# One gate/up pair of three FFNs moved from plain products to seven products

## The chip, the core and the metric

The kernel runs on one core of a Trainium2 chip. The time is that of one execution on the device in microseconds (us); of several executions the median counts. The engines named below are TensorE (PE; its weight loads are PEld), VectorE (DVE), ScalarE (ACT), GpSimd (POOL) and SyncE (SP).

## What is computed

Two layers, each with a half-step FFN, a mixer (a gated linear recurrence and a windowed attention side by side) and a second half-step FFN. Only the FFNs matter here:

```
def rms_norm(x, gain):
    y = x * rsqrt(mean(x * x, axis=-1, keepdims=True) + 1e-6)
    return y * gain

def swiglu(h, w_gate, w_up, w_down):
    return (silu(h @ w_gate) * (h @ w_up)) @ w_down

for l in range(2):
    h = rms_norm(x, gn[0])
    x = x + 0.5 * rms_norm(swiglu(h, w_ffn1_gate[l], w_ffn1_up[l], w_ffn1_down[l]), gn[1])
    ...                                          # the mixer
    h = rms_norm(x, gn[4])
    x = x + 0.5 * rms_norm(swiglu(h, w_ffn2_gate[l], w_ffn2_up[l], w_ffn2_down[l]), gn[5])
```

x is 512 tokens by 1024 channels, gate and up are 1024 by 2816, down is 2816 by 1024, all float32. There are four FFNs.

## The kernel before

**Precision.** Every float32 operand is split into two float32r parts, `hi` and `lo`, and a product is three matmuls: hi with hi, hi with lo, lo with hi (`mm3`, all on line 115 through `mm`). Weights are the stationary operand of the gate/up products, tokens the moving one.

**Pairs.** The 2816 columns of gate and of up are 22 blocks of 128; block j of gate and block j of up are a pair, whose 512 results each become one block of the hidden vector. A pair is made in one of two ways.

- Plain: eight blocks of 128 channels for gate and eight for up, three matmuls each, 512 tokens wide: 48 matmuls. The first two pairs run together in `quad`, further ones through two calls of `project`, and `gated` (lines 909 and 910) makes silu(gate) times up.
- Seven products (`sevenths`, line 850): the channels and the tokens are halved, gate and up are the two column blocks, and seven products of quarter size take the place of eight. Each is four blocks of three matmuls, 256 tokens wide: 84 matmuls in all. Their order on PE is product 1, 2, 5, 7, 6, 3, 4. Results are put together on DVE: line 874 after product 6, lines 876 and 881, line 882 after product 4; ACT's Silu of line 894 and DVE's line 895 then give the hidden block.

`PLAIN` says how many pairs are plain in the three FFNs behind the first (the first has `FIRST`); the others take seven products. `fast` runs the pairs from `PLAIN` to 21 in a loop.

**Weights.** `Stream` brings them. A raw block of 128 by 1024 (512 KB) comes by SP's queue into one of four buffers (`w32`) and is split into `whi` and `wlo`, for which there are six buffers each. A plain pair is two items of kind u, whose `lo` DVE computes (line 331). A pair of seven products is four items out of two raw blocks:

- a (products 1 and 2): a raw block. ACT writes hi (line 324) and minus w into lo (line 328), then POOL issues a DMA that adds w to it (line 329).
- b (products 5 and 7): DVE makes two sums of weights (lines 311 and 312), ACT casts hi, DVE computes lo (line 331).
- c (products 6 and 4): the same with lines 317 and 318.
- d (product 3): half a raw block, its lo by ACT and a DMA of 256 KB, like a's.

Each item is prepared some items ahead of its use (`AHEAD` is 3).

**Tokens.** The products 5, 6, 3 and 7 need sums of token quarters. `Pre.sums` makes those of one pair of channel blocks: line 563 twice, lines 458 to 465, and a split of two tiles (ACT line 400, DVE line 401). Four calls fill `x56` and `x37`, and product 5 of the first pair needs all four. Two are called after `quad`, one ahead of each further plain pair.

**Order.** PE's instructions run in the order of the program. That of DVE, ACT, POOL and SP is chosen by the tile framework's scheduler when the kernel is built, apart from those under `pin`. An engine works through its list in order, and an instruction that waits holds up all behind it.

Of the kernel before, what the change touches and what calls it, by code (L numbers as in the profile page):

```python
# [33 lines left out]
    head=2600.0, level=1720.0, chunks=1270.0, blocks=350.0, norm=2370.0, gate=8000.0,  # L34
    values=1200.0, scores=2000.0, exp=9000.0, shares=4500.0, turn=1900.0, turned=3000.0, rest=1200.0, lent=3500.0, apart=4000.0, block=2000.0, pair=4000.0, att0=1260.0, att1=12300.0,
)
W32, WS, AHEAD, TAIL, PLAIN, FIRST, EARLY, LATE = 4, 6, 3, 4, 4, 7, 4, 8
TURN = 0
LEAD = 8
ORDER = ("p1", "p6", "p2", "p7", "p5", "p4", "p3")  # L40
# [5 lines left out]
def trunk(ctx: ExitStack, tc: tile.TileContext, xin, wall, gains, lbT, hgain, sinks, c_dist, c_mask, c_ident, out):  # L46
# [16 lines left out]
    def big(dt=F32, shape=None):  # L63
        return sb.tile(shape or [P, S], dt, tag="s", name=nm("s"), bufs=SLOTS)
# [750 lines left out]
    def quad(pre, halves):  # L815

        o = [acc() for _ in range(4)]
        blocks = {}
        ws.pinned = halves
        for half in (0, 1) if halves else (None,):  # L820
            c = WHOLE if half is None else HALF[half]
            for k in range(KT):
                order.until(lambda: pre.have[half or 0] > k)
                for j in range(4):
                    if (k, j) not in blocks:
                        blocks[k, j] = ws.next(uses=2 if halves else 1)
                    wmm(o[j][:, c], blocks[k, j], cut(pre.h[k], c), k == 0, k == KT - 1)
            ws.pinned = False
        return o

    def project(pre):
        o = acc()
        for k in range(KT):
            wmm(o, ws.next(), pre.h[k], k == 0, k == KT - 1)
        return o
# [49 lines left out]
    def fast(pre, a, start):  # L885
        def early():
            if j == FT - 1:
                for i in range(EARLY):
                    a[i] = split(a[i])

        for j in range(start, FT):
            m = sevenths(pre, early)
            z = big(F32, [P, 2, H2])
            nc.scalar.activation(out=m[:, 0:2, :], in_=m[:, 0:2, :], func=AF.Silu)  # L894
            nc.vector.scalar_tensor_tensor(z, m[:, 0:2, :], -1.0, m[:, 2:4, :], op0=ALU.mult, op1=ALU.mult)
            a.append(z.rearrange("p i t -> p (i t)"))

    def ffn(l, n, pre, nxt, halves=True):
        a = []

        def gated(og, ou):
            z, u = big(), big()
            if first:
                pin(nc.vector.tensor_tensor(z, og, pre.rb, op=ALU.mult))
                nc.scalar.activation(out=z, in_=z, func=AF.Silu)
                nc.vector.tensor_tensor(u, ou, pre.rb, op=ALU.mult)
                nc.vector.tensor_tensor(u, u, z, op=ALU.mult)
            else:
                nc.scalar.activation(out=z, in_=og, func=AF.Silu)
                pin(nc.vector.tensor_tensor(u, ou, z, op=ALU.mult))  # L910
            a.append(u)

        first = isinstance(pre, First)
        o = quad(pre, halves)
        if first:
            o.append(project(pre))
            order.until(lambda: pre.rb is not None)
        if not first:
            pre.sums()
            pre.sums()  # L920
        for j in range(2):
            gated(o[2 * j], o[2 * j + 1])
        if first:
            gated(o[4], project(pre))
            for j in range(3, FIRST):
                if j > 3:
                    order.until(lambda: pre.laid)
                    pre.sums()
                if j == 4:
                    pre.sums()  # L930
                gated(project(pre), project(pre))
            fast(pre, a, FIRST)
        else:
            for j in range(2, PLAIN):
                pre.sums()
                gated(project(pre), project(pre))
            fast(pre, a, PLAIN)
        return down(a, FT, l, n + 1, nxt, True)
# [349 lines left out]
    pre = First()  # L1288
# [69 lines left out]
    for l in range(DEPTH):  # L1358
        pre = ffn(l, 0, pre, (l, 2), halves=l > 0)
        pre = mixer(l, pre, (l, 4))  # L1360
        pre = ffn(l, 4, pre, (l + 1, 0) if l + 1 < DEPTH else None)
# [81 lines left out]
```

## Time and profile before

| | |
|---|---|
| median of 3 runs | 2113.25 us (2112.46 to 2113.26) |
| the profiled execution | 2114.98 us, of which the profile's span is 2113.2 us |
| busy share of the span | PE 99%, PEld 89%, DVE 73%, ACT 53%, POOL 7% |
| granted TensorE clock | 0.998 |
| DMA | 298.36 MB, 141 GB/s in the mean |

In the profile L115 is line 115 of the kernel. A row of the timeline has the start in us from the span's start, the length in us, engine, line, operation, the tile written, the tile read, and in brackets the idle time ahead of it with what ended it. A matmul's length includes its way through the array, so the distance between starts counts, not the length.

### The profile page before, as it was taken

Reading aid. Unit: us, or ns where it says so; the run is one execution under the profiler, and the core shown is the slowest. Engines: PE = TensorE matmul, PEld = TensorE weight load, DVE = VectorE, ACT = ScalarE, POOL = GpSimd, SP = SyncE. Lnnn points to the kernel's source line nnn. Section 1 sums busy time; section 2 is a strip of 40 time slices with the busy share of each in tenths; the row PEclk is TensorE's granted clock in tenths of the full one; section 3 lists DMA queues with packets and bytes.
Section 4 is the critical chain, followed back from the end, with each engine's and each line's share of the span. In section 5 each row is a group of like instructions: output and inputs, shape, how many; then the busy total and the mean of one; then the engine's idle time right before and its main releaser. Section 6 shows DMA issues by size and latency. Waiting matters only on the chain.

```text
span 2113.2 us, 35244 instructions
## 1 busy us (share of the span) xinstructions
PE 2101.1 (99%) x13549; PEld 1875.3 (89%) x13549; DVE 1551.0 (73%) x2705; ACT 1124.9 (53%) x1900; POOL 154.6 (7%) x188
## 2 busy tenths in 40 slices
PE   9999999999999999999999999999999999999998
PEld 7899988887888999998899998888778989999987
DVE  5777886767676777779587778767686767777884
ACT  6555554446445555556355556454554545555562
POOL 0111000000000011110001110000000000111000
PEclk9999999999999999999999999999999999999999
DMA  7577754321237357774437775632122553677651
GB/s 234 150 181 181 188 146 137 106 70 61 70 100 209 120 125 175 180 194 125 160 109 175 181 185 150 189 116 95 51 71 70 135 185 110 154 182 181 183 165 45
DMA packets 148072, 298.36 MB, mean 141 GB/s; under 512 B 16992, under 2 KB 74816, under 8 KB 147904
## 3 DMA queue, kind: packets, MB, share of 16 engines
q1 hardware_dynamic: 122416, 228.16, 32.8%
q0 software_dynamic: 25344, 67.91, 18.5%
q8 instruction: 106, 1.74, 0.3%
q14 instruction: 62, 0.51, 0.1%
q10 hardware_dynamic: 144, 0.05, 0.0%
HBM read 213.43 MB, written 14.73 MB: 108 GB/s over the span
## 4 chain that ended last, share of the span: by engine, by line
PE 81%; DVE 9%; ACT 5%; issue 2%; DMA 2%; SPq 1%; ACTq 0%; DVEq 0%
PE acc L115 60%; PE aux L115 19%; ACT whi L324 2%; DMA w<-wall 2%; PE aux L125 1%; DVE s L401 1%; DVE wlo L331 1%; DVE wlo L286 1%; PE acc L125 1%; ACT s L400 1%; ACT m L894 1%; ACT wlo L328 1%; SPq L241 1%; DVE tt L268 0%; DVE w L267 0%
## 5 line engine op out<-in xcount | busy, mean ns | idle before, releaser
L115 PE MATMUL acc<-s,whi 128*128 128x256 f32 (+1 forms) x4968 | 1069.9, 312 | 1.7 <-ACT whi L324 0.9
L115 PEld LDWEIGHTS acc<-s,whi 128*128 128x128 f32 x4968 | 809.9, 191 | 54.5 <-issue 2.1
L115 PE MATMUL acc<-s,wlo 128*128 128x256 f32 (+1 forms) x2484 | 770.5, 310 | 0.1
L115 PEld LDWEIGHTS acc<-s,wlo 128*128 128x128 f32 x2484 | 474.5, 191 | 25.9 <-DVE wlo L331 0.4
L324 ACT CAST whi<-w 128x1024 fp32r<-128x1024 f32 (+1 forms) x341 | 317.4, 949 | 252.2 <-PE aux L115 103.4
L115 PE MATMUL acc<-whi,s 128*128 128x512 f32 x1264 | 413.6, 393 | 0.0
L324 ACT CAST whi<-tt 128x1024 fp32r<-128x1024 f32 x154 | 161.7, 1050 | 341.4 <-DVE tt L318 188.9
L331 DVE TENSOR_TENSOR wlo<-w,whi 128x1024 fp32r<-128x1024 f32 (+1 forms) x181 | 218.5, 1216 | 134.8 <-ACT whi L324 128.4
L115 PEld LDWEIGHTS acc<-whi,s 128*128 128x128 f32 x1264 | 237.0, 188 | 55.7 <-issue 3.2
L331 DVE TENSOR_TENSOR wlo<-tt,whi 128x1024 fp32r<-128x1024 f32 x154 | 188.2, 1222 | 102.5 <-ACT whi L324 102.5
L115 PE MATMUL acc<-wlo,s 128*128 128x512 f32 x632 | 246.8, 391 | 1.0 <-DVE wlo L286 1.0
L329 POOL DMA_DIRECT2D wlo<-w x160 | 138.2, 865 | 1266.3 <-ACT wlo L328 856.7
L115 PE MATMUL aux<-s,whi 128*128 128x256 f32 x1232 | 225.1, 283 | 0.0
L115 PE MATMUL aux<-whi,s 128*128 128x512 f32 x592 | 196.8, 390 | 0.0
L115 PEld LDWEIGHTS aux<-s,whi 128*128 128x128 f32 x1232 | 192.2, 192 | 0.0
L115 PE MATMUL aux<-s,wlo 128*128 128x256 f32 x616 | 174.4, 283 | 0.1
L115 PEld LDWEIGHTS acc<-wlo,s 128*128 128x128 f32 x632 | 118.7, 188 | 25.8 <-DVE wlo L286 2.4
L115 PEld LDWEIGHTS aux<-whi,s 128*128 128x128 f32 x592 | 111.1, 188 | 22.9
L328 ACT ACTIVATE wlo<-w 128x1024 fp32r<-128x1024 f32 (+1 forms) x160 | 129.9, 845 | 0.0
L400 ACT CAST s<-s 128x512 fp32r<-128x512 f32 (+1 forms) x164 | 88.6, 581 | 65.9 <-DVE s L459 60.6
L115 PEld LDWEIGHTS aux<-s,wlo 128*128 128x128 f32 x616 | 118.3, 192 | 0.3 <-DMA wlo<-w 0.3
L115 PE MATMUL aux<-wlo,s 128*128 128x512 f32 x296 | 115.2, 389 | 0.0
(185 smaller groups left out, 2136.6 us busy)
## 6 DMA issues: line engine op xcount, KB each, us to landing
w<-wall SPq DMA_DIRECT2D x267, 512.0 KB, 3.7
wlo<-w POOLq DMA_DIRECT2D x83, 512.0 KB, 5.5
w<-wall SPq DMA_DIRECT2D x288, 128.0 KB, 3.1
wlo<-w POOLq DMA_DIRECT2D x77, 256.0 KB, 3.3
x_d<-s SPq DMA_DIRECT2D x48, 256.0 KB, 2.1
s<-x_d SPq DMA_DIRECT2D x48, 256.0 KB, 5.5
w<-wall SPq DMA_DIRECT2D x34, 256.0 KB, 2.9
s<-wall SPq DMA_DIRECT2D x64, 128.0 KB, 3.5
```

The source lines that it names most:

```text
L115: nc.tensor.matmul(o, lhsT, rhs, start=start, stop=stop)
L125: nc.tensor.transpose(o, src, ident)
L241: nc.sync.dma_start(w.rearrange("p (m c) -> p m c", m=4) if c is None else w[:, c], a)
L286: nc.vector.tensor_tensor(it.lo[:, h[c]], w[c], it.hi[:, h[c]].bitcast(F32), op=ALU.subtract)
L324: i = nc.scalar.copy(it.hi[:, c], w[:, c])
L328: nc.scalar.mul(it.lo[:, c], w[:, c], -1.0)
L329: nc.gpsimd.dma_start(it.lo[:, c].bitcast(F32), w[:, c], accum_op=ALU.add)
L331: nc.vector.tensor_tensor(it.lo[:, c], w[:, c], it.hi[:, c].bitcast(F32), op=ALU.subtract)
L400: nc.scalar.copy(hi, src)
L401: nc.vector.tensor_tensor(lo, src, hi.bitcast(F32), op=ALU.subtract)
L894: nc.scalar.activation(out=m[:, 0:2, :], in_=m[:, 0:2, :], func=AF.Silu)
```

## The change

`PLAIN` goes from 4 to 3: in each of the three FFNs behind the first, pair 3 takes seven products. Two calls of `Pre.sums` that stood ahead of two plain pairs now both stand ahead of the only one.

```
-W32, WS, AHEAD, TAIL, PLAIN, FIRST, EARLY, LATE = 4, 6, 3, 4, 4, 7, 4, 8
+W32, WS, AHEAD, TAIL, PLAIN, FIRST, EARLY, LATE = 4, 6, 3, 4, 3, 7, 4, 8
...
             for j in range(2, PLAIN):
-                pre.sums()
+                while len(pre.x56) < min(4, 2 * j):
+                    pre.sums()
                 gated(project(pre), project(pre))
             fast(pre, a, PLAIN)
```

The stream of weights follows from `PLAIN` (`ws.plain(min(2 * p, 8))`, `ws.pairs(FT - p)`): two items u fewer and one set a, b, c, d more in each of the three.

## The prediction

> **What bounds the kernel now.** I read the page first, then the chain that ended last, then the timeline of each engine around the place of the change in the second FFN.
>
> ```profile
> PE 2101.1 (99%) x13549; PEld 1875.3 (89%) x13549; DVE 1551.0 (73%) x2705; ACT 1124.9 (53%) x1900; POOL 154.6 (7%) x188
> PE 81%; DVE 9%; ACT 5%; issue 2%; DMA 2%; SPq 1%; ACTq 0%; DVEq 0%
> wlo<-w POOLq DMA_DIRECT2D x83, 512.0 KB, 5.5
> wlo<-w POOLq DMA_DIRECT2D x77, 256.0 KB, 3.3
> ```
>
> PE is never idle to speak of, so matmuls that go are worth their full time, as long as what feeds PE keeps its lead. The last two rows are the accumulating DMAs that finish `wlo` of items a and d: 5.5 and 3.3 us from POOL's issue to landing.
>
> ```profile
> 725.83 43.37 PE acc L115 x276
> 769.19 2.88 PE aux L115 x24
> 772.07 7.20 PE acc L115 x60
> ...
> 740.05 0.63 PE L115 MATMUL acc<-s,whi 128*128 128x512 f32 x2
> 761.84 0.40 PE L115 MATMUL acc<-s,whi 128*128 128x256 f32 x2
> ```
>
> The first three rows are of the chain: quad, both plain pairs and the first seven products pass without a gap, and a pair of seven products takes 7.20 + 2.88 = 10.08 us (84 matmuls, 0.12 us apart). The other two are of PE's timeline: the plain pairs 2 and 3 run from 740.05 to 761.84, 10.9 us each (48 matmuls, 0.227 us apart, 10.88).
>
> The lead is the question. This is DVE and ACT in the steady part of the third FFN:
>
> ```profile
> 1160.17 0.68 DVE L311 TENSOR_TENSOR tt<-w,w 128x512 f32<-128x512 f32 x1
> 1162.57 1.23 DVE L331 TENSOR_TENSOR wlo<-tt,whi 128x1024 fp32r<-128x1024 f32 x1 [1.12 <-ACT whi L324]
> 1163.71 0.68 DVE L317 TENSOR_TENSOR tt<-tt,w 128x512 f32<-128x512 f32 x1
> 1164.43 0.69 DVE L318 TENSOR_TENSOR tt<-tt,w 128x512 f32<-128x512 f32 x1
> 1165.04 0.68 DVE L874 TENSOR_TENSOR m<-acc,s 128x512 f32<-128x512 f32 x1
> 1169.12 0.61 ACT L894 ACTIVATE m<-m 128x512 f32<-128x512 f32 x1
> 1169.64 0.35 ACT L864 COPY s<-acc 128x256 f32<-128x256 f32 x1
> 1170.38 0.69 DVE L311 TENSOR_TENSOR tt<-w,w 128x512 f32<-128x512 f32 x1
> 1238.31 0.19 PEld L115 LDWEIGHTS acc<-s,wlo 128*128 128x128 f32 x1 [0.22 <-DMA wlo<-w]
> ```
>
> DVE and ACT need 10.21 us for one round (L311 at 1160.17, again at 1170.38), PE 10.08. So PE gains 0.13 us a pair on its feeders, and near the end of that FFN it has used the lead up: the last row is a weight load waiting for item a's DMA. The feeders live on the lead with which they enter the loop.
>
> **The saving.** Three pairs go from 10.88 to 10.08 us: 3 x 0.80 = 2.4 us less on PE. The Trainium skill, "TensorE: Matmul & The Clock Gate", section "Back-to-back issue gap", gives N / 2.4 + 2.5 ns between isolated warm matmuls; by that the pairs would take 10.36 and 9.17 us and the saving would be 3.6 us; the rows' 0.227 and 0.12 us decide.
>
> **The token sums.** In the new order the third and fourth step follow each other. One step starts at 743.44 and the next work at 747.76:
>
> ```profile
> 743.44 1.28 DVE L563 TENSOR_TENSOR s<-s,s 128x512 f32<-128x512 f32 x2
> 746.54 1.29 DVE L401 TENSOR_TENSOR s<-s,s 128x512 fp32r<-128x512 f32 x2 [0.23 <-ACT s L400]
> 747.76 0.69 DVE L311 TENSOR_TENSOR tt<-w,w 128x512 f32<-128x512 f32 x1
> 756.22 0.68 DVE L317 TENSOR_TENSOR tt<-tt,w 128x512 f32<-128x512 f32 x1
> 756.93 0.69 DVE L318 TENSOR_TENSOR tt<-tt,w 128x512 f32<-128x512 f32 x1
> 757.71 1.05 ACT L324 CAST whi<-tt 128x1024 fp32r<-128x1024 f32 x1 [0.52 <-DVE tt L318]
> 758.67 0.61 ACT L324 CAST whi<-w 128x512 fp32r<-128x512 f32 x1
> 758.79 1.23 DVE L331 TENSOR_TENSOR wlo<-tt,whi 128x1024 fp32r<-128x1024 f32 x1 [1.17 <-ACT whi L324]
> 759.19 0.63 ACT L328 ACTIVATE wlo<-w 128x512 fp32r<-128x512 f32 x1
> 759.72 1.04 ACT L324 CAST whi<-w 128x1024 fp32r<-128x1024 f32 x1
> 760.66 1.05 ACT L328 ACTIVATE wlo<-w 128x1024 fp32r<-128x1024 f32 x1
> 760.11 0.86 POOL L329 DMA_DIRECT2D wlo<-w  x1 [19.70 <-DVE wlo L331]
> 762.01 0.86 POOL L329 DMA_DIRECT2D wlo<-w  x1 [1.04 <-PE acc L115]
> ```
>
> That is 4.32 us a step, so the fourth ends at 747.76 + 4.32 = 752.08. Seven products now start at 740.05 + 10.88 = 750.93, and product 5 at 753.81: the sums are 1.7 us early and cost nothing by themselves. But c's sums (L317, L318) stand behind them, and behind c on ACT's list stand d and the next pair's a.
>
> **The first pair of each FFN.** Moved from 756.22 to 752.08, the chain of the rows above keeps its distances: c's lo is done at 752.08 + 2.57 + 1.23 = 755.88, needed at 750.93 + 5.76 = 756.69: 0.8 us early. d's DMA is issued at 760.11 - 4.14 = 755.97 and lands 3.3 us later at 759.27; product 3 starts at 750.93 + 7.20 and needs lo at its third matmul, 758.37: 0.9 us late. The next a is issued at 762.01 - 4.14 = 757.87 and lands 5.5 us later at 763.37; the second pair needs it at 761.01 + 0.24 = 761.25: 2.1 us late, which includes d's 0.9. Before, both had about five us to spare, since one more pair was still plain. So the first pair costs 2.1 us and saves 0.8.
>
> **The rounds behind it.** With so little lead the scheduler builds another loop. The lists in the built program, by line (b, c, d, a are items):
>
> ```
> before, every round    DVE  311 312 331b 317 318 874 876 331c 881 882 895
>                        ACT  864 cast-b cast-c cast-d cast-a mul-d mul-a 894
> after, every third     DVE  311 312 874 331b 317 876 318 881 882 331c 895
>                        ACT  864 cast-b cast-c cast-d mul-d 894 | cast-a mul-a
> after, the other two   DVE  311 312 331b 317 874 318 876 881 331c 882 895
>                        ACT  864 cast-b cast-c cast-d mul-d cast-a mul-a 894
> ```
>
> In every third round L874 comes ahead of b's lo. It waits for product 6 of the running pair, and behind it on DVE wait b and c, behind c on ACT d, the Silu and only then a.
>
> ```profile
> 779.31 0.69 DVE L874 TENSOR_TENSOR m<-acc,s 128x512 f32<-128x512 f32 x1 [0.24 <-PE acc L115]
> ```
>
> This row shows L874 released by PE: 0.04 us after product 6 of the pair from 772.07 (+7.20); matmul starts stand some 0.15 us ahead of the chain's, so I count 0.2. From a pair's start S, with the distances of the rows: L874 at 7.4, L331b 8.0, L317 9.15 (+1.14), L876 9.75, L318 10.35, cast c 11.15 (+0.78), cast d 12.1, mul d 12.6, Silu 13.15 (+0.53), cast a 13.7 (+0.52), mul a 14.65, POOL's issue 16.0 (+1.35), landing 21.5. The pair after next starts at S + 20.16 and needs it at 20.4: 1.1 us late, and PE waits. d of that round is issued at 13.5, lands at 16.8 and is needed at 10.08 + 7.44 = 17.5: in time. In the round behind it DVE and ACT follow at once: L895 13.8, L311 14.4, cast b 15.9 (behind a), L331b 17.0, L318 19.35, cast c 20.15, cast a 22.15, issue 24.45, landing 29.95; needed at 20.16 + 1.1 + 10.08 + 0.24 = 31.6, so in time; the third has some 1.2 us left. So one wait of 1.1 us for each third round, 5 in an FFN (rounds 3, 6, 9, 12, 15, or 2, 5, 8, 11, 14; the round 0 finds the second pair already delayed).
>
> **The sum.** For each FFN -0.8 + 2.1 + 5 x 1.1 = +6.8 us; three give +20.4. The durations are of an execution of 2114.98 us with a span of 2113.2; the median of the runs shown is 2113.25, and I add to that: 2133.5 us. No row shows the changed end of the loop; the waits for `whi` and `wlo` at the quarter products of `down` behind it are fractions of a us now, and I take 0 with 1 us per FFN either way. Items of u that go (two L331, L909, L910) are hidden before and after.
>
> The unknown is how long a's DMA takes when it is issued apart from d's, with SP's raw loads beside it. The single issues behind 760.11 that stand apart:
>
> ```profile
> wlo<-w POOLq DMA_DIRECT2D x1, 512.0 KB, 4.7
> wlo<-w POOLq DMA_DIRECT2D x1, 512.0 KB, 6.3
> wlo<-w POOLq DMA_DIRECT2D x1, 512.0 KB, 5.2
> ...
> 772.90 0.86 POOL L329 DMA_DIRECT2D wlo<-w  x1 [1.87 <-ACT wlo L328]
> 783.47 0.86 POOL L329 DMA_DIRECT2D wlo<-w  x1 [1.03 <-ACT wlo L328]
> ```
>
> (issued at 762.01, 772.90 and 783.47). At 4.7 an FFN's sum is -0.8 + 1.3 + 5 x 0.3 = +2.0, in all +6; at 6.3 it is -0.8 + 2.9 + 5 x 1.9 = +11.6, in all +35. I take the median over all 83, 5.5.
>
> **The rivals.**
>
> *Only the first pair stalls.* The rounds find their lead again, because PE's own wait gives it to them. For it: a wait of 2.1 us is twice what a third round lacks. Against it: that round's delay starts from PE's product 6, so it moves with PE. 2113.25 + 3 x (2.1 - 0.8) = 2117.2 us, 0.17.
>
> *Not slower: the DMAs land sooner.* If the adding DMA of 512 KB, with POOL less busy, landed within 761.25 - 757.87 = 3.4 us, neither the first pair nor any round would wait for a (a third round only from 20.4 - 16.0 = 4.4 us on). d's 0.9 us would be left, or 0 if it too were 0.9 us faster: 2113.25 - 2.4 = 2110.9 to 2113.6 us. Against it stand the 4.7, 5.2 and 6.3. The Trainium skill, "DMA: Bandwidth & Descriptors", section "Anatomy of one DMA — SWDGE (gpsimd) path", fits such a DMA as 2.0 us plus bytes over 436 GB/s, by which it would be an estimated 3.2 us and this rival would be the forecast; the trace's 4.7 to 6.3 disagree. 0.13, since another program shifts what the DMAs share their engines with.
>
> *Worse than forecast.* The third rounds issue d 2.4 us ahead of a, so the raw loads that d's landing frees run beside a: like the 6.3 case. 2113.25 + 35 = 2148 us and above, 0.10.
>
> *The forecast*, with a between about 5 and 6 us: 2119 to 2146 us, 0.60.
>
> **How the numbers follow.** The range runs from 2113.5 to 2148: it holds the forecast and the first rival with 1 us per FFN of the loop's end either way (2117.2 less 3, rounded down), and ends where the worse case begins; what it leaves out is that case and the second rival, some 0.2. 0.2% of the time, about what a measurement can tell from no change, is 4.2 us, the bound at 2117.5. Slower has the forecast, the worse case and under half of the first rival: 0.77. Same has the rest of that rival and the second: 0.21. Faster than 2109.0 would need more than the whole saving: 0.02.
>
> **What would show it.** Right: the chain's pieces between 725 and 772 in one plain pair less; a PEld row with `<-DMA wlo<-w` of about 1 us at product 3 of the first pair or about 2 us in sum by the start of the second pair; the same wait of about 1 us every third pair, fifteen in all; DVE's L874 idle ahead for some 2 us in those rounds; pairs otherwise 10.08 us. Wrong: no such waits, or waits on DVE's `x56` tiles (L401), or PE waits that grow each pair (then the round, not the DMA, is the bound).

## The result, and the profile after

The changed kernel takes 2140.60 us (median of 4 runs, 2139.73 to 2144.43), the kernel before in the same job 2113.02 us (4 runs). The ratio is 1.0133, with a 95% interval from 1.0121 to 1.0145: slower by 27.6 us. The profiled execution took 2141.42 us, with a span of 2139.3 us (before: 2113.2).

Four lines of the page after:

```profile
PE 2103.7 (98%) x13657; PEld 1879.1 (88%) x13657; DVE 1563.1 (73%) x2729; ACT 1129.8 (53%) x1915; POOL 159.8 (7%) x194
PE 56%; issue 22%; DVE 4%; DMA 2%; POOL 2%; ACT 2%; SPq 0%; POOLq 0%; DVEq 0%; ACTq 0%
wlo<-w POOLq DMA_DIRECT2D x86, 512.0 KB, 5.5
wlo<-w POOLq DMA_DIRECT2D x80, 256.0 KB, 3.3
```

The shares of busy time hardly moved. In the chain that ended last PE's part fell from 81 to 56%, since through most of the three loops it now runs along POOL's list of issues, and the time between two issues counts as "issue". That points at the adding DMAs, but is no measure of the cost. The medians of their transfers are as long as before.

The waits of PE's weight loads name the cost. The columns are total us, times, longest us:

```profile
PEld acc L115 <- DMA wlo<-w: 23.0, 17, 2.5
PEld aux L115 <- DMA wlo<-w: 3.5, 3, 1.6
PEld acc L115 <- ACT s L400: 1.4, 1, 1.4
```

There are twenty waits for the adding DMAs, 26.5 us in all. Before, there were two such waits, 0.2 and 0.3 us (the longer one in the first FFN). The place is seen when each loop of seven products is taken as a window, from its first matmul to the first of `down` (length, then PE's busy time and matmuls, those of PEld, DVE, ACT and POOL, the granted clock, the DMA share and GB/s). First the three loops of the kernel before, then those of the changed one:

```profile
761.84:943.27 181.43, 181.43 (x1514) 181.43 (x1512) 138.98 (x195) 103.93 (x144) 29.34 (x34) 1.00 0.75 180
1106.86:1288.57 181.71, 181.69 (x1514) 181.49 (x1512) 138.57 (x195) 103.53 (x143) 29.36 (x34) 1.00 0.75 181
1805.13:1986.57 181.44, 181.44 (x1514) 181.43 (x1513) 139.05 (x195) 104.10 (x144) 29.32 (x34) 1.00 0.74 181
```

```profile
751.42:951.70 200.28, 193.04 (x1598) 191.82 (x1597) 149.44 (x211) 112.77 (x158) 31.93 (x37) 1.00 0.74 177
1103.72:1304.40 200.68, 193.34 (x1597) 191.91 (x1596) 149.55 (x212) 112.86 (x158) 31.95 (x37) 1.00 0.73 173
1811.59:2012.73 201.14, 193.29 (x1598) 191.87 (x1596) 149.48 (x211) 112.69 (x158) 31.90 (x37) 1.00 0.74 175
```

Eighteen pairs of 10.08 us are 181.44, nineteen are 191.52. The loops before lose 0.3 us together, the loops after 602.10 - 3 x 191.52 = 27.5 us. The difference of the spans is 26.1: 27.5 - 0.3 lost in the loops, less 2.4 saved, and 1.3 outside them.

Now one third round of the second FFN, from DVE, ACT, POOL, the DMAs issued in it, and PE's weight loads:

```profile
790.76 0.69 DVE L874 TENSOR_TENSOR m<-acc,s 128x512 f32<-128x512 f32 x1 [1.67 <-ACT whi L324]
791.37 1.22 DVE L331 TENSOR_TENSOR wlo<-tt,whi 128x1024 fp32r<-128x1024 f32 x1
793.70 0.68 DVE L318 TENSOR_TENSOR tt<-tt,w 128x512 f32<-128x512 f32 x1
```

```profile
794.47 1.05 ACT L324 CAST whi<-tt 128x1024 fp32r<-128x1024 f32 x1 [4.30 <-DVE tt L318]
796.48 0.61 ACT L894 ACTIVATE m<-m 128x512 f32<-128x512 f32 x1
797.00 1.03 ACT L324 CAST whi<-w 128x1024 fp32r<-128x1024 f32 x1
797.93 1.06 ACT L328 ACTIVATE wlo<-w 128x1024 fp32r<-128x1024 f32 x1
```

```profile
799.28 0.86 POOL L329 DMA_DIRECT2D wlo<-w  x1 [1.55 <-ACT s L864]
```

```profile
wlo<-w POOLq DMA_DIRECT2D x1, 512.0 KB, 5.6
```

```profile
804.97 0.19 PEld L115 LDWEIGHTS acc<-s,wlo 128*128 128x128 f32 x1 [1.31 <-DMA wlo<-w]
836.73 0.19 PEld L115 LDWEIGHTS acc<-s,wlo 128*128 128x128 f32 x1 [1.47 <-DMA wlo<-w]
868.36 0.19 PEld L115 LDWEIGHTS acc<-s,wlo 128*128 128x128 f32 x1 [1.34 <-DMA wlo<-w]
```

DVE is idle 1.67 us ahead of L874, and b's lo stands behind it. (The row names the cast as what it waited for, but that had ended at 790.17. PE's product 6 was the later one.) ACT then waits 4.30 us for c's sums, the Silu stands ahead of a, and a's DMA is issued at 799.28. The pair's first matmul started at 783.30, so that is S + 16.0, the figure of the prediction. It lands 5.6 us later, 1.31 us too late. The next such waits are 31.8 and 31.6 us behind, which is three pairs and one wait.

### The profile page after: what moved, and what is told of

Its sections match the earlier page's. It is cut to its first block, busy times and chain, and to the rows that moved or that the text cites. A ratio compares the mean times of both kernels' runs of the same rounds, so it can differ in the third digit from the quotient of the medians.

```text
span 2139.3 us, 35560 instructions
## 1 busy us (share of the span) xinstructions
PE 2103.7 (98%) x13657; PEld 1879.1 (88%) x13657; DVE 1563.1 (73%) x2729; ACT 1129.8 (53%) x1915; POOL 159.8 (7%) x194
## 4 chain that ended last, share of the span: by engine, by line
PE 56%; issue 22%; DVE 4%; DMA 2%; POOL 2%; ACT 2%; SPq 0%; POOLq 0%; DVEq 0%; ACTq 0%
PE acc L115 40%; PE aux L115 14%; POOL wlo L329 2%; DMA wlo<-w 1%; PE aux L125 1%; DVE s L401 1%; DMA w<-wall 1%; PE acc L125 1%; DVE wlo L286 1%; ACT s L400 0%; ACT whi L281 0%; DVE w L267 0%; DVE tt L268 0%; DVE s L276 0%; DVE w L277 0%
## 5 line engine op out<-in xcount | busy, mean ns | idle before, releaser
L324 ACT CAST whi<-tt 128x1024 fp32r<-128x1024 f32 x160 | 167.8, 1048 | 374.8 <-DVE tt L318 254.7
L331 DVE TENSOR_TENSOR wlo<-w,whi 128x1024 fp32r<-128x1024 f32 (+1 forms) x175 | 211.0, 1216 | 130.3 <-ACT whi L324 129.4
L331 DVE TENSOR_TENSOR wlo<-tt,whi 128x1024 fp32r<-128x1024 f32 x160 | 195.7, 1223 | 87.5 <-ACT whi L324 83.3
L329 POOL DMA_DIRECT2D wlo<-w x166 | 143.3, 865 | 1285.3 <-ACT wlo L328 887.9
L115 PE MATMUL aux<-s,whi 128*128 128x256 f32 x1280 | 234.0, 283 | 0.0
L115 PEld LDWEIGHTS aux<-s,whi 128*128 128x128 f32 x1280 | 199.6, 192 | 0.0
L115 PE MATMUL aux<-s,wlo 128*128 128x256 f32 x640 | 181.5, 284 | 2.9 <-DMA wlo<-w 2.9
L328 ACT ACTIVATE wlo<-w 128x1024 fp32r<-128x1024 f32 (+1 forms) x166 | 139.6, 849 | 0.0
L400 ACT CAST s<-s 128x512 fp32r<-128x512 f32 (+1 forms) x164 | 88.6, 581 | 71.9 <-DVE s L459 67.8
L115 PEld LDWEIGHTS aux<-s,wlo 128*128 128x128 f32 x640 | 122.8, 192 | 3.5 <-DMA wlo<-w 3.5
```

Of the source, the lines that this page charges most:

```text
L115: nc.tensor.matmul(o, lhsT, rhs, start=start, stop=stop)
L324: i = nc.scalar.copy(it.hi[:, c], w[:, c])
L328: nc.scalar.mul(it.lo[:, c], w[:, c], -1.0)
L329: nc.gpsimd.dma_start(it.lo[:, c].bitcast(F32), w[:, c], accum_op=ALU.add)
L331: nc.vector.tensor_tensor(it.lo[:, c], w[:, c], it.hi[:, c].bitcast(F32), op=ALU.subtract)
L400: nc.scalar.copy(hi, src)
```

## The experiments

The ratios are against runs of the kernel before on the same chip, each with its 95% interval.

### e1: the sums alone

```
 PLAIN = 4
-                pre.sums()
+                while len(pre.x56) < min(4, 2 * j):
+                    pre.sums()
```

> The kernel before with one part of the change alone: PLAIN stays 4, and both late steps of token sums stand ahead of pair 2. The lists that the scheduler builds for DVE and ACT in the rounds of seven products stay those of the kernel before. Theory (the sums back to back cost nothing, the lists of the rounds and the lost lead cost all): 2113.0 us within 0.7, no wait on wlo of more than 0.5 us at the start of a loop. Rival (the sums back to back are a cost of their own, since c and d and a of the next pair stand behind them): a wait at the start of each loop, 1 to 2 us for each of three FFNs, 2116 to 2119 us.

2112.14 us against 2112.20, ratio 1.0000 (0.9991 to 1.0008). The one wait of a weight load for `wlo` is of 0.20 us, at 1236, in the third FFN. The sums back to back cost nothing. This run is also the reference for the stages below, since it ran beside e2 to e4.

### e2: L874 back in its old place

```
+    def behind(i, prev):                     # order on one engine, no wait
+        tc.add_manual_dep(i.ins, prev.ins.name, ...NoSync...)
...
-        nc.vector.tensor_tensor(m[:, 0:4:2, :], ...)              # L874
+        i = nc.vector.tensor_tensor(m[:, 0:4:2, :], ...)
+        if held: behind(i, ws.c2)                                 # c2: c's second sum
```

> The changed kernel, with L874 held behind c's second sum (L318) on DVE in the three loops, which gives the list of the kernel before in every round (311 312 331b 317 318 874 876 331c 881 882 895); nothing else moves. Theory (L874 ahead of b's lo makes a's transfer late in every third round): the fifteen later waits go and the first pairs' 1.60, 2.34 and 1.52 us stay, less the 2.4 us saved: 2113.0 + 5.5 - 2.4 = 2116 us, from 2114 to 2119. Rival (the rounds of DVE and ACT, 10.2 us against PE's 10.08, are too slow without the lead, in whatever order): 19 x 0.13 = 2.5 us more for each FFN, 2123 us or above, with waits in nearly every pair. Rival (the transfer alone is too slow, in whatever order): no better than 2135 us.

2117.68 us, ratio 1.0027 (1.0017 to 1.0037): 5.5 us over the kernel before, where the changed kernel is 27.6 over it. So the list with L874 ahead of b's lo was worth some 22 of the 27.6 us. One thing more moved, though the expectation says that nothing else does: in the trace ACT's list, too, is now the same in every round, with item a ahead of the Silu (L894), where the changed kernel has the Silu ahead of a in every third round. By the distances of the prediction the Silu makes up 0.55 us of such a round's delay. e7 has L874 ahead of b's lo and a ahead of the Silu, and so tells the two apart. The loops and the weight loads' waits:

```profile
749.00:941.80 192.80, 191.80 (x1597) 191.60 (x1596) 148.92 (x210) 112.14 (x157) 31.85 (x37) 1.00 0.75 181
1095.02:1289.26 194.24, 192.40 (x1598) 191.71 (x1597) 150.12 (x213) 114.41 (x160) 31.87 (x37) 1.00 0.74 181
1794.33:1988.15 193.82, 192.27 (x1597) 191.66 (x1596) 149.66 (x212) 113.20 (x158) 31.82 (x37) 1.00 0.75 181
```

```profile
PEld aux L115 <- DMA wlo<-w: 3.7, 4, 1.4
PEld acc L115 <- DMA wlo<-w: 2.1, 3, 1.0
```

The regular waits are gone. Five of the seven that are left, 5.0 us, stand at the first pairs (the other two are 0.21 and 0.59 us, late in the loops). The rival of slow rounds would have given 2123 or more and falls as the main cause, as does that of the transfer alone.

### e3: half the transfer

```
+                    c = h[0] if it.kind == "a" else c
                     nc.gpsimd.dma_start(it.lo[:, c]..., w[:, c], accum_op=ALU.add)
```

> The changed kernel with a's adding DMA cut to the first half of its columns, 256 KB instead of 512 (the other half of a's lo keeps minus w, so the output is another); the lists of DVE and ACT stay as in the changed kernel. Theory (in a third round a is issued at S + 16.0 and has 4.4 us to land; 512 KB need 5.5, 256 KB need 3.3 to 4): no wait in the third rounds, 0.9 to 1.6 us at product 3 of each first pair, 2113.0 - 2.4 + 3 x (0.9 to 1.6) = 2113 to 2116 us. Rival (the issue is late, not the landing: DVE and ACT do not keep up): 2135 to 2141 us.

2120.65 us, ratio 1.0039 (1.0026 to 1.0052): 20 us under the changed kernel, but 5 over what I expected.

```profile
PEld aux L115 <- DMA wlo<-w: 6.7, 7, 2.3
PEld acc L115 <- ACT s L401: 3.2, 2, 2.4
```

No row `PEld acc ... <- DMA wlo<-w` is left: with half the bytes a is in time everywhere, on the same lists. So the issue at S + 16.0 was late only by what the landing takes. The expectation missed what lies beside a: d's waits were 2.9 us at the first pairs, as expected, and 3.8 us more further on (2.25 of them at one place, which e4 explains), and `down` waited 2.4 us at its start for a split of ACT (L400 of the kernel before). A kernel without lead pays for these too.

### e4: the start of each loop as well

```
                 # pair 2, on top of e2
+                pre.sums()
+                ws.most = 4
+                og = project(pre)
+                pre.sums()
+                ws.most = 3
+                gated(og, project(pre))
```

> The changed kernel with L874 held behind L318 as in e2, and the start of each loop mended too: the third step of sums, then the gate half of pair 2 with the lookahead at 4 items, the fourth step, the up half with 3. On ACT's list the casts of d and of the next a then stand ahead of the casts of the fourth step, so both transfers are issued about 4 us earlier. Theory (late transfers are all that the change costs): no waits on wlo are left, and the whole saving of 2.4 us shows: 2110.6 us, from 2109.5 to 2112. Rival (the fourth step's sums, now behind c's, come too late for product 5 of the first pair): a wait on an x56 tile (L401) of 1 to 2.5 us in each FFN, 2113 to 2118 us.

2116.67 us, ratio 1.0023 (1.0013 to 1.0032). This expectation failed, by 6 us. The mechanism did what it should, and no first pair waits any more. Yet the loops lose 5.5 us (192.59, 193.84 and 193.59 long), in other places. One of them, by ACT, POOL and PEld:

```profile
1209.36 0.63 ACT L331 ACTIVATE wlo<-w 128x512 fp32r<-128x512 f32 x1
```

```profile
1212.24 1.75 POOL L332 DMA_DIRECT2D wlo<-w  x2 [9.41 <-ACT wlo L331]
```

```profile
1215.57 0.19 PEld L115 LDWEIGHTS aux<-s,wlo 128*128 128x128 f32 x1 [1.26 <-DMA wlo<-w]
```

POOL's row holds the issues of d and of a. ACT was done with d at 1209.99, but POOL issued its DMA at 1212.24, 2.25 us behind, where the median is 0.3. The two other waits of more than 1 us in the loops (1.02 and 1.45) follow two issues that came 0.97 us behind. Every trace has these three late issues, and they are always the 57th, the 106th and the 155th of POOL's adding DMAs, 49 apart. The kernel before has lead and hardly feels them. Nor can e4 make them good, since the round of DVE and ACT is longer than a pair (L900 here is L895 of the changed kernel):

```profile
1202.24 0.69 DVE L900 SCALAR_TENSOR_TENSOR s<-m 128x512 f32<-128x512 f32 x1 [1.25 <-ACT m L899]
1212.44 0.69 DVE L900 SCALAR_TENSOR_TENSOR s<-m 128x512 f32<-128x512 f32 x1 [1.25 <-ACT m L899]
```

10.20 us apart, against 10.08, with DVE idle for 1.25 us ahead of L900. So the rival of slow rounds, dropped after e2, has a share after all: not for the twenty waits, but for the lead that never comes back.

### e5: the Silu ahead of a's second half

```
                     i = nc.scalar.mul(it.lo[:, c], w[:, c], -1.0)         # L328
+                    if it.kind == "a" and ws.silu is not None:
+                        behind(i, ws.silu)                                # the Silu, L894
```

> e4 with one thing more: in the three loops ACT's Silu (L894 of the changed kernel) stands ahead of a's second half, the multiplication by -1 (L328), so that DVE's L895, and with it the next round, need not wait for it. In e4 no wait on wlo was left at the start of a loop; three were left inside the loops (1.02, 1.26 and 1.45 us), each some 6 us behind one of POOL's issues that came 0.97, 2.25 and 0.97 us behind ACT's part instead of the usual 0.2, and the rounds of DVE and ACT took 10.2 us, so PE found no lead there. Theory (the feeders' rounds are longer than a pair, so neither lost lead nor a hiccup is made good): with 0.5 us less in the round, a lead of 1.5 us or more builds up, the 0.97s are absorbed, at most 0.5 us of the 2.25 is left, and the loops take 19 x 10.08 us: 2111 us, from 2110 to 2113, 1 us or more faster than the kernel before. Rival (the rest of e4's loss lies elsewhere, at down's start and in the start of the program): 2115 to 2117 us as e4.

2115.06 us, ratio 1.0014 (1.0005 to 1.0022): 1 to 2 us better than e4 and not the 5 or more that I expected. The round fell to 9.7 us, but in the rounds in which a gives way it is later itself, and its transfer became longer. The transfers of a issued at 763.29 and 782.72, with the raw load that was issued beside each (the waits behind them were 0.98 and 1.10 us), and a wait at the third pair of the third FFN:

```profile
wlo<-w POOLq DMA_DIRECT2D x1, 512.0 KB, 6.3
w<-wall SPq DMA_DIRECT2D x1, 512.0 KB, 5.9
...
wlo<-w POOLq DMA_DIRECT2D x1, 512.0 KB, 8.2
w<-wall SPq DMA_DIRECT2D x1, 512.0 KB, 5.4
```

```profile
1115.60 0.19 PEld L115 LDWEIGHTS acc<-s,wlo 128*128 128x128 f32 x1 [1.49 <-DMA wlo<-w]
```

e5 has such a wait at the third pair of each loop (0.98, 1.49, 1.96 us). A faster round alone is not the cure if it is bought with a's place.

### e6: the same in the kernel before

The edit is that of e5.

> The kernel before with the Silu ahead of a's multiplication by -1 in the three loops, and nothing else. Theory (its rounds live on the lead of the fourth plain pair, which lasts through the loop but for 0.2 to 0.3 us): nothing to gain, 2112.2 us within 1. Rival (the Silu's place is worth time by itself, whatever the number of plain pairs): as much faster as e5 is than e4, 2107 to 2109 us.

2112.18 us against 2112.12, ratio 0.9998 (0.9989 to 1.0007). There is no gain, as the theory had it, but the traces show that this is a sum of two shifts. Beside e1 the three loops are 1.5 us longer in all (182.07, 182.45 and 181.68 us, with three waits for `wlo`), and the stages behind them some 2 us shorter (116.03, 116.03 and 125.79 us).

### e7: L874 ahead of b in every round

```
+        ws.most = 4 if start < FIRST else AHEAD      # once, ahead of the loop
         for j in range(start, FT):
+            if j == FT - 1:
+                ws.most = AHEAD
```

> The changed kernel with the lookahead at 4 items in the three loops, for which the scheduler puts L874 ahead of b's lo in every round (311 312 874 876 331b 317 881 318 882 331c 895) and not in every third. Theory (this place of L874 is what makes a late): replayed by the rows' distances with landings of 5.2 to 5.7 us, a wait of 0.4 to 0.8 us at nearly every pair, 10 to 13 us for each loop, in all 2113 + 28 to 36: 2140 to 2148 us. Rival (the place of L874 is a by-product, and the time hangs on the lookahead: a fourth item ahead makes a earlier): waits at the first pairs only, 2117 us or below.

2145.56 us, ratio 1.0160 (1.0146 to 1.0174).

```profile
PEld acc L115 <- DMA wlo<-w: 24.3, 40, 2.0
PEld aux L115 <- DMA wlo<-w: 5.6, 8, 1.6
```

```profile
793.50 0.19 PEld L115 LDWEIGHTS acc<-s,wlo 128*128 128x128 f32 x1 [0.44 <-DMA wlo<-w]
803.97 0.19 PEld L115 LDWEIGHTS acc<-s,wlo 128*128 128x128 f32 x1 [0.34 <-DMA wlo<-w]
```

Where every round has the list, most pairs wait (40 waits for an a among 57 pairs), for 0.2 to 1.0 us mostly, in place of 1.4 us at every third. This is the pattern that the distances of the rows gave, and the time is inside the range. In the trace a stands ahead of the Silu on ACT in every round, so L874's place makes a late by itself, and with e2 this is seen from both sides.

### e8: L895 one pair later

```
                 # on top of e4, without e5
         c = ws.whole()
+        if late is not None:
+            behind(late(), ws.b2)     # the last pair's L895, behind b's second sum
+        m = sb.tile(...)              # was at the head of sevenths
...
-            nc.vector.scalar_tensor_tensor(z, ...)                       # L895
+            late = (lambda z=z, m=m: times(z, m)) if ... else None
```

> e4, without e5's edit, with the last step of a pair (L895 of the changed kernel, the product of the Silu and the other half) issued one pair later, so that on DVE it stands behind b's two sums of the pair after (314 315 899 320 334b 321 334c 879 883 888 889 by this kernel's lines). In e4 and e5 DVE stood idle 1.25 us in each round until ACT's Silu was done, with L895 and the next round behind it; now the sums run in that time, and the distance of d's and a's issues stays 1.9 us (in e5 it was 2.9 and a's transfers took 6.3, 5.1 and 8.2 us in the first rounds, where e4's took 5.3, 4.9 and 5.2). Theory (a round longer than a pair is why no lead comes back): the round falls from 10.2 to about 9 us where it is free, a lead of some us builds up in the first rounds, POOL's late issues (0.97, 2.25, 0.97 us) are absorbed, the loops take 19 x 10.08 us within 0.5 and the whole saving is left: 2110.0 to 2111.5 us, 1 to 2 us under the kernel before. Rival (a's transfer, not the round, is what holds PE: with more lead it meets more raw loads and takes longer, as in e5): waits of 1 to 2 us at the third pairs stay, 2113 to 2116 us.

2106.98 us against 2111.83, ratio 0.9977 (0.9968 to 0.9986): faster than both kernels, and than I expected. The loops:

```profile
749.48:940.99 191.51, 191.51 (x1597) 191.51 (x1596) 152.90 (x215) 119.56 (x159) 31.84 (x37) 1.00 0.79 187
1092.77:1284.28 191.51, 191.51 (x1598) 191.51 (x1597) 153.67 (x217) 120.24 (x161) 31.85 (x37) 1.00 0.78 187
1788.99:1980.50 191.51, 191.51 (x1597) 191.51 (x1596) 151.67 (x213) 119.43 (x159) 31.81 (x37) 1.00 0.78 186
```

Each is 19 x 10.08 us, with no wait at all. Three rows of DVE show how, and a row of POOL that its late issue is still there:

```profile
1193.76 0.69 DVE L889 TENSOR_TENSOR m<-aux,s 128x512 f32<-128x512 f32 x1 [1.00 <-PE aux L115]
1194.37 0.68 DVE L314 TENSOR_TENSOR tt<-w,w 128x512 f32<-128x512 f32 x1
1195.57 0.69 DVE L899 SCALAR_TENSOR_TENSOR s<-m 128x512 f32<-128x512 f32 x1
```

```profile
1203.04 0.86 POOL L332 DMA_DIRECT2D wlo<-w  x1 [7.63 <-issue]
```

The sums of the next b (L314) run while ACT does the Silu, and L899 (L895 of the changed kernel) finds it done. Now DVE waits for PE (1.00 us a round), and PE for nothing. In this list c's lo, too, stands ahead of L874, where e4 has it behind L876, and no run keeps the two apart. Two points of the expectation were off. The distance of d's and a's issues did not stay at 1.9 us but became 3.5, and the landings rose (medians of 5.8 and 3.8 us on this page): with lead that does not matter. And the stages behind the loops, up to the next product of 256 tokens or the end, are shorter too: 116.04, 116.03 and 125.6 us, against 116.96, 116.49 and 126.4 in e1, and the loops 0.4 in all. That makes the second half of the 4.9 us.

### e9 and e10: whose gain is it

e9 is the kernel before (PLAIN 4) with e8's loop, and e10 is the changed kernel with L895 one pair later and nothing else.

> The kernel before (PLAIN 4) with e8's edits to the loops: the same list for DVE, L895 one pair later. e8 came out at 2107.0 us, 4.9 under the kernel before, where 2.4 of saving were to be had; its loops take 191.51 us each (19 x 10.08) and the stages behind the loops 116.04, 116.03 and 125.6 us, where e1's loops took 181.44, 181.80 and 181.43 (18 x 10.08 = 181.44) and its stages behind them 116.96, 116.49 and 126.4. Theory (the pair is worth its 2.4 us when the lead is there; the other 2.5 us come from the lead at the end of the loops and do not need the change): 2112 - 0.4 - 2.2 = 2109.4 us, from 2108.5 to 2110.5, so that the change is worth -2.4 us between e9 and e8. Rival (the list is worth nothing to the kernel before, whose loops hardly waited): 2111.5 to 2112.5 us, and the change on this loop would be worth -4.9 us.

> The changed kernel with L895 one pair later as in e8, and nothing else of e2 or e4: L874 is not held, and the start of each loop is that of the changed kernel. The list built for 44 of the rounds is 320 334b 321 334c 879 881 886 887 314 315 897 by this kernel's lines, with L874 (here 879) behind b, c and c's lo; no third rounds are left. Theory (lead cures the rounds, the first pairs keep their late d and a): 2107.0 + 1.60 + 2.34 + 1.52 = 2112.5 us, from 2111 to 2114, the same as the kernel before. Rival (without e4's start the loops never come to the lead): waits inside the loops, 2116 us or more.

e9 takes 2110.03 us, ratio 0.9987 (0.9978 to 0.9996), e10 2113.08 us, ratio 1.0002 (0.9993 to 1.0011). Both are inside what was expected. From e9 to e8 only the pair and e4's start differ, and the ratios against the kernel before differ by 0.0010, 2.1 us, though their intervals overlap. The traces are sharper: from one and the same matmul ahead of the second FFN's plain pairs to the loop's end it is 97.32 + 181.43 = 278.75 us in e9 and 86.44 + 191.51 = 277.95 in e8, 0.80 less, which for three is the 2.4 us of the prediction. e10's five waits for `wlo` are all at the first pairs (1.63; 1.37 and 0.91; 0.58 and 1.00, sum 5.5 us), and 2106.98 + 5.5 = 2112.5 us.

## Why the prediction was right, point by point

The direction, the mechanism and its places came as forecast. The size was 27.6 us and not 20.4, and the time lies inside the range.

- **The saving, 2.4 us.** Shown between e9 and e8, at 0.80 us a pair. By the gap for isolated matmuls that the Trainium skill gives in "TensorE: Matmul & The Clock Gate", section "Back-to-back issue gap", it is an estimated 3.6 us. These traces disagree and keep the gaps of the rows, 0.227 and 0.12 us.
- **The token sums, no cost.** Shown by e1.
- **The first pair, 2.1 us each, 6.3 in all.** Measured 1.60, 1.38 + 0.96 and 0.55 + 0.97: 5.5. POOL's issues in the second FFN:

```profile
756.06 0.86 POOL L329 DMA_DIRECT2D wlo<-w  x1 [20.95 <-DVE wlo L331]
757.96 0.86 POOL L329 DMA_DIRECT2D wlo<-w  x1 [1.04 <-ACT s L864]
```

  I had 755.97 and 757.87, so the chain moved as a whole. The landings were 4.3 and 4.9 us for 3.3 and 5.5, so in the second FFN the whole wait fell on d and none on a.
- **The rounds behind it, 15 x 1.1 = 16.5 us.** Fifteen waits came, 21.0 us together, 1.40 in the mean. **This is the term that was mis-sized.** The issue at S + 16.0 was right. Over the fifteen a landed after 5.7 us in the mean where I had put 5.5, and with so little to spare 0.2 us of landing is a fifth of the wait. One wait in the fourth FFN was 2.46 us, for which I had nothing; there a landed after 6.8 us. The 5.5 was the median of a kernel that in its loops mostly issues a 0.9 us behind d; in these rounds it is 2.4 us behind.
- **The loop's end, 0 with 1 us either way.** -0.7, +1.5 and -0.1 us from loop to loop. The 1.5 is `down`'s wait of 1.38 us for `s` of L400, with one of 0.51 for L401 behind it.
- **The sum.** 26.5 us of waits - 2.4 is 24.1, for 20.4 predicted. The rest of the 26.1 between the spans is 0.7 that the loops lose beyond these waits, the loop's ends (0.7) and the start of the program (0.5). The medians of the runs lie 27.6 apart, 1.5 more than the two profiled spans. (The forecast adds up to 2133.65 and not to 2133.5 us, which changes nothing.)
- **The rival of the first pair alone** needed the rounds to find lead through PE's wait. They did not. e10 is the kernel in which they do, and there this rival's waits are all that is left.
- **The rival of sooner landings** needed 3.4 us. The landings were 4.9 and 5.6. The 3.2 us estimated from the Trainium skill, "DMA: Bandwidth & Descriptors", section "Anatomy of one DMA — SWDGE (gpsimd) path", were not seen in any profile here: no adding DMA of 512 KB landed within 4.5 us, and the medians are 5.3 to 5.8 us (e3, with only six of them, aside).
- **The worse case** had d's landing set raw loads free beside a. With issues 2.4 us apart the fifteen landings were 5.2 to 5.8 us and once 6.8: against 5.5 it rose by 0.3 us at most, not by 0.8, but for that one. Longer ones exist (up to 8.2 us in e5, at 2.9 us apart). That raw loads make them long is not shown, since no run changes the raw loads alone.

What the prediction did not see is why the lead is lost for good. It priced the waits one by one, and by that e4 should have been without loss. Two things outside the sum take what the lists do not. One is the round of 10.20 us against a pair of 10.08, which the prediction read but left out of the sum; the other is POOL's three late issues. In e8, with DVE's idle time of 1.25 us a round gone, neither costs anything any more.

One reading of the prediction was wrong by this. It took the wait at 1238.31 in the kernel before for lead that is used up. The a it waits for is POOL's 107th issue, held up behind the late 106th:

```profile
1231.80 1.75 POOL L329 DMA_DIRECT2D wlo<-w  x2 [10.36 <-ACT s L864]
```

The row holds d's and a's issue, 2.25 and 1.90 us behind ACT's parts. At the pair after, a landed again some 2 us ahead of its use. The lead does shrink, from about 5 us at the start of a loop to 1.1 to 1.6 at its end, but it is not used up.

What stays open: why the scheduler builds the three lists that it builds, what holds POOL at its late issues, and what lengthens a's transfers.

## What to carry to other kernels

Work that PE can do in less time is worth its difference only if what feeds PE keeps its lead: here 0.8 us a pair were saved and a lead of some 5 us went with the pair. Compare the feeders' round with the pair that it feeds (10.20 and 10.08 us): if it is longer, every late start stays, and the first thing to mend is the idle time in the round, here an instruction that waits for another engine with the next round behind it. When a change of sizes makes a scheduler build other lists, read the lists first: the one in which an instruction that waits stands ahead of those that others need cost some 22 us by e2's comparison.

## What the runs showed of the hardware that was not expected

- In all twelve traces POOL issues its 57th, 106th and 155th adding DMA late: 0.97, 2.25 and 0.97 us behind ACT's part, where the median is 0.29. The count stays and the place does not: the kernels with PLAIN at 3 issue two more in each loop, and yet the same three are late (the 155th at 1950.15 in the kernel before, 145 us into its loop, and at 1943.43 in the changed one, 132 us into it). In e8 the row of the 106th says `<-issue`: POOL waited for nothing that the profile shows.
- An adding DMA of 512 KB took from 4.5 to 8.9 us, with the same bytes and the same kind of source. Within the three loops its median rises with the distance from d's issue: 5.2 us when it is 1.9 us behind (e2 and e4), 5.6 at 2.4 (the changed kernel), and 6.5, 6.9 and 6.3 at 3.5 (e8, e9 and e10). It is no plain rule, since at 0.9 us behind (the kernel before) it is 5.5.
